# Low parts of the weights by an accumulating DMA in every fourth slab, in place of a VectorE subtraction

## The chip, the cores and the metric

One core of a Trainium2 chip runs the kernel. The metric is device time in microseconds (us) of one execution, lower is better. Engines are called as the profile calls them: PE (TensorE matmul), PEld (its weight loads), DVE (VectorE), ACT (ScalarE), POOL (GpSimd) and SP (SyncE, which here only issues DMAs).

## What is computed

One layer of a streaming encoder on 256 tokens of width 2048, all float32: a half-step feed-forward (SwiGLU), a mixer of latent attention and gated linear attention, cross-attention to 256 memory tokens, and a second half-step feed-forward.

```python
def swiglu(h, w_gate, w_up, w_down):
    return (jax.nn.silu(h @ w_gate) * (h @ w_up)) @ w_down
...
        x = x + 0.5 * swiglu(rmsnorm(x, ffn1_norm[l]), ffn1_w_gate[l], ffn1_w_up[l], ffn1_w_down[l])
        h = rmsnorm(x, mix_norm[l])
        z = h @ w_in[l]
...
        x = x + jnp.concatenate([o_mla, o_gla], axis=-1) @ w_out[l]
        x = x + memory_cross_attention(rmsnorm(x, mem_attn_norm[l]), rmsnorm(mem, mem_norm[l]), ...)
        x = x + 0.5 * swiglu(rmsnorm(x, ffn2_norm[l]), ffn2_w_gate[l], ffn2_w_up[l], ffn2_w_down[l])
```

D_MODEL is 2048 and D_FF 5632, so nearly all the time goes into products of 256 rows with large weight matrices, each weight read once from HBM.

## The kernel before

**Products in two parts.** To keep float32 accuracy, each operand is split into a high part (the value cast to float32r) and a low part (the value less its high part). A product is three matmuls: high x high, weights' low x high, weights' high x low. `gemm` (from L113) holds the activations' k-tiles of 128 as the stationary operand and streams 512 columns of weights; a k-tile of 1024 weight columns is worked off in 12 matmuls (two blocks of 128 tokens, two chunks of 512 columns, three products). In each pair the matmul with `wh` (high) stands directly ahead of the one with `wl` (low).

**Slabs.** `slab` (from L89) loads weights and splits them. For columns 1024 wide a slab is two k-tiles, called tile A and tile B below: 1 MB in one `raw` buffer, loaded by SP (L97; in the gate and up products two DMAs of 512 KB, in the others one of 1 MB). For each tile ACT casts `raw` to `wh` (L108) and DVE subtracts `wh` from `raw` into `wl` (L109):

```python
self.last_act = nc.scalar.copy(out=wh, in_=src)
self.last_dve = nc.vector.tensor_tensor(out=wl, in0=src, in1=wh.bitcast(F32), op=ALU.subtract)
```

**Buffers set the lead.** There are three `raw` buffers, and four each of `wh` and `wl`; a tile of 1024 columns takes one of each. So the split of a tile can begin when PE has finished the tile four before it, and PE has three more tiles to do before it needs the new one. A `raw` buffer is free for SP's load of three slabs later when both readers of tile B are done.

**Order.** The Tile framework traces the program and a scheduler fixes each engine's order of instructions; every engine works in that order, and semaphores hold an instruction until its operands and buffers are ready. SP's queue holds the loads, POOL's queue holds small operations for the norms (factors of 128 x 2 to 128 x 8 elements) and a few DMAs of small tables at the start and ahead of the mixer (`b_gate`, L462).

**Course of the program.** `ffn` runs 11 gate/up products of 8 slabs and four down products of 10 or 12 slabs; then comes the mixer (some narrower weights, and attention work woven in between the k-tiles), the cross-attention, and `ffn` again. The first product is special: its first two slabs hold one tile each, and the input's columns are loaded and transposed in between.

Of the kernel before, what the change touches and what calls it, by code (L numbers as in the profile page):

```python
# [10 lines left out]
F32 = mybir.dt.float32  # L11
# [4 lines left out]
ALU = mybir.AluOpType  # L16
AX = mybir.AxisListType

P = 128
# [5 lines left out]
CW = 512  # L25
EPS = 1e-6

H = 8
NOPE, ROPE, VD = 128, 64, 128
# [22 lines left out]
class Kernel:  # L52
    def __init__(self, ctx, tc, io):
        self.tc, self.nc, self.io = tc, tc.nc, io
        pool = lambda name, bufs, **k: ctx.enter_context(tc.tile_pool(name=name, bufs=bufs, **k))
        self.const = pool("const", 1)
        self.keep = pool("keep", 1)
        self.wraw = pool("wraw", 3)
        self.wspl = pool("wspl", 4)
        self.tmp = pool("tmp", 3)  # L60
        self.small = pool("small", 1)
        self.acc = pool("acc", 4, space=bass.MemoryType.PSUM)
        self.ps = pool("ps", 4, space=bass.MemoryType.PSUM)
        self.n_small = 0

# [8 lines left out]
    def rsqrt_mean(self, ss, n, scale=None):  # L74
        """(ss * scale + EPS) ** -0.5, elementwise on [P, n] (Pool)."""
        nc = self.nc
        ms = self.sm([P, n])
        nc.gpsimd.tensor_scalar(out=ms, in0=ss, scalar1=scale, scalar2=EPS, op0=ALU.mult, op1=ALU.add)
        r = self.sm([P, n])
        nc.gpsimd.tensor_tensor(out=r, in0=ms, in1=self.mhalf[:, :n], op=ALU.pow)  # L80
        return r
# [7 lines left out]
    def slab(self, segs, k0, nk, per):  # L89
        """k-tiles k0.. of the segments' columns: a (high, low) pair [P, width] for each; per of them at a time."""  # L90
        nc = self.nc
        width = sum(w for _, _, w in segs)
        flat = self.wraw.tile([P, 4 * CW], F32, name="raw")
        raw = flat[:, :nk * width].rearrange("p (j n) -> p j n", j=nk)
        off = 0
        for w, c0, n in segs:
            nc.sync.dma_start(  # L97
                out=raw[:, :, off:off + n],
                in_=w[k0 * P:(k0 + nk) * P, c0:c0 + n].rearrange("(j p) n -> p j n", p=P),
            )  # L100
            off += n
        parts = []
        for j in range(0, nk, per):
            m = min(per, nk - j)
            wh = self.wspl.tile([P, 2 * CW], F32R, name="wh")[:, :m * width]
            wl = self.wspl.tile([P, 2 * CW], F32R, name="wl")[:, :m * width]
            src = flat[:, j * width:(j + m) * width]
            self.last_act = nc.scalar.copy(out=wh, in_=src)  # L108
            self.last_dve = nc.vector.tensor_tensor(out=wl, in0=src, in1=wh.bitcast(F32), op=ALU.subtract)  # L109
            parts += [(wh[:, i * width:(i + 1) * width], wl[:, i * width:(i + 1) * width]) for i in range(m)]  # L110
        return parts

    def gemm(self, x, segs, chunks, ks, ahead=None, side=()):  # L113
        """x(k, b) -> (high, low) [P, P]; out[b][c] = sum_k x(k, b).T @ w[k][:, chunk c].

        side: generators of other work, a step of each traced after each k-tile."""
# [12 lines left out]
        while i < n:  # L129
# [9 lines left out]
            # one accumulator after the other in the last slab, so that they end apart  # L139
# [22 lines left out]
    def split_t(self, src, dst, j0, b, nj, g=None):  # L162
        """src [P tokens, nj * P] to dst's k-tiles j0.. for token block b; g: their columns in gains."""
# [31 lines left out]
    def norm_chunk(self, src, ht, ss, n, b, g, sq=True):  # L195
        """One [P, CW] chunk of the residual stream: its part of h.T and its sum of squares."""
        self.split_t(src, ht[n], 0, b, 4, g + 4 * n)
        if sq:
            self.sum_sq(src, ss[:, b, n:n + 1], CW)
# [32 lines left out]
    def load_rows(self, names, queue):  # L232
        """Norm weights, 128 to a row."""
# [9 lines left out]
    def turn_rows(self, rows, first, n):  # L243
        """... and to columns of gains."""
        t = self.bank()
        self.nc.tensor.transpose(out=t[:, :n], in_=rows[:n], identity=self.ident[:n, :n])
        return self.nc.vector.tensor_copy(out=self.gains[:, first:first + n], in_=t[:, :n])
# [5 lines left out]
    def setup_mix_body(self, pool):  # L253
# [7 lines left out]
        # products of the q and k norms' weights over the dimensions that aren't rotated  # L261
# [3 lines left out]
        # 0 where a key's chunk is not after the query's, within one block of 128  # L265
# [3 lines left out]
        # suffix[s, t] = 1 where s > t in the same chunk of 64; ends[s, c] = 1 where s is in chunk c  # L269
# [14 lines left out]
        # rotary tables: x * ta + swapped(x) * tb, each with the norm's weights in it  # L284
# [11 lines left out]
        # angles less whole turns (taken off part by part, each part exact), cos as a sine a quarter turn on  # L296
# [49 lines left out]
    def rotate(self, x, out, q, b, n):  # L346
        """x [P, n, ROPE] rotated (norm's weights included) into out [P, n, ROPE]."""
# [110 lines left out]
    def latent_input(self, lat, gate, x, z, r1, eds, dec):  # L458
        """Low-rank q and kv and the rotary key (in z), the gates' decays."""
# [25 lines left out]
        def steps():  # L485
# [27 lines left out]
            # log-sigmoid: min(y, 0) - log(1 + exp(-|y|))  # L513
# [7 lines left out]
            # the decay from a position to its chunk's end, and the chunk's  # L521
# [18 lines left out]
    def gla_qk(self, out, r1, gqt, eds):  # L540
        """q of gated linear attention, transposed; its k times the decay, in place of the decay."""
# [14 lines left out]
    def gla_states(self, gqt, eds, dec, gv, states, sso):  # L556
        """Chunk by chunk: states, and their outputs in place of gv; sums of squares of these."""
# [41 lines left out]
    def gla_gate(self, out, on, sso, r1, ogt):  # L599
        """Outputs of gated linear attention, normed and gated, transposed and split."""  # L600
# [33 lines left out]
    def latent_group(self, pool, g, z, r1, omt):  # L634
        """Four heads of latent attention, in two pairs: q, k and v, then what is left to do with them."""
# [34 lines left out]
        def steps():  # L670
            nsc = []
            ssq, ssk = self.sm([P, NB, 4]), self.sm([P, NB, 4])
            for b in range(NB):
# [12 lines left out]
                # minus the factor of the scores: both norms of q and the softmax's scale  # L686
# [10 lines left out]
                # k's factors: of the part from the low rank, of the rotary part  # L697
# [47 lines left out]
    def attend(self, scores, nscales, finish, causal, pts=None):  # L745
        """Heads one after the other, each a step behind the one before: scores and softmax; transposed; finish."""
# [11 lines left out]
    def soft_max(self, scores, nscale, causal):  # L758
        """One head's softmax over the keys: a tile [queries, keys] for each block of queries."""
# [19 lines left out]
    def soft_max_t(self, ss, pt, causal):  # L779
        """... transposed: pt's columns are (keys' block, query), without (1, block 0) when causal."""  # L780
# [9 lines left out]
    def weigh(self, v, pt, ot, k, causal):  # L790
        """One head's output, transposed and split, as k-tile k of ot."""
# [11 lines left out]
    def memory(self, pool, mt, mss):  # L803
        """mem, transposed and split, and its chunks' sums of squares."""
# [8 lines left out]
    def cross(self, pool, ht, mt, rm, r1, done):  # L813
# [18 lines left out]
        def head_norm(row, b, r, r2, scale):  # L832
            """The factors that turn a block's raw columns into normed ones, by head, times scale."""
# [60 lines left out]
    def run(self):  # L894
# [22 lines left out]
        def ahead(k):  # L917
            """Columns of x before the k-tiles that need them."""
# [64 lines left out]
```

## Time and profile before

| what | value |
|---|---|
| time, median of 2 runs | 1962.15 us (1961.65 and 1962.65) |
| span of the profiled execution (first to last instruction) | 1960.3 us |
| median less span | 1.9 us |
| PE busy | 1944.5 us, 99% |
| DVE busy | 1015.1 us, 52% |
| ACT busy | 903.7 us, 46% |
| POOL busy | 58.8 us, 3% |
| 16 DMA engines busy, SP's loads | 54.4% of the span |
| granted TensorE clock, mean | 0.999 |

How to read it: a busy share is that of an engine over the whole span. PE rows show the matmul's whole length, which overlaps with its neighbours; the distance from start to start is what a matmul costs in a row of many. A wait is put down to the engine whose work ended last before the waiting instruction began.

### The profile page before, as it was taken

How to read it: one execution, taken by the hardware profiler on the slowest of the kernel's cores; microseconds unless marked ns; L12 is line 12 of the kernel's file. 1: busy time of each engine (PE TensorE's matmuls, PEld its weight loads, DVE VectorE, ACT ScalarE, POOL GpSimd, SP SyncE). 2: the span in 40 equal slices, each digit the busy share in tenths (PEclk: the TensorE clock that was granted, in tenths of full speed). 3: DMA queues.
4: the chain of work that ended last, by engine and by line, in shares of the span. 5: the costliest groups of instructions: out<-in, count | busy, mean ns of one | idle time of the engine just before them, and what ended most of it. 6: DMA issues, size and time to landing. Idle time of an engine off the chain costs nothing.

```text
span 1960.3 us, 22343 instructions
## 1 busy us (share of the span) xinstructions
PE 1944.5 (99%) x8712; PEld 1583.4 (81%) x8712; DVE 1015.1 (52%) x1272; ACT 903.7 (46%) x1277; POOL 58.8 (3%) x114
## 2 busy tenths in 40 slices
PE   8999999999999999999999999999999999999999
PEld 6888888888888888788778878888888888888887
DVE  5555454444444455555566656444454445544443
ACT  5444443334444344665556666444444334444432
POOL 2000000000000000120100020000000000000000
PEclk9999999999999999999999999999999999999999
DMA  7555555555555555544335544655555555555563
GB/s 263 184 186 189 185 190 184 192 193 183 185 191 193 181 184 171 181 154 155 126 130 203 185 155 137 206 186 184 189 192 185 183 190 193 178 191 189 193 205 117
DMA packets 148074, 356.04 MB, mean 182 GB/s; under 512 B 11018, under 2 KB 11120, under 8 KB 147968
## 3 DMA queue, kind: packets, MB, share of 16 engines
q1 hardware_dynamic: 147360, 354.07, 54.4%
q8 instruction: 68, 1.11, 0.2%
q0 software_dynamic: 608, 0.55, 0.2%
q14 instruction: 38, 0.31, 0.0%
HBM read 352.48 MB, written 2.10 MB: 181 GB/s over the span
## 4 chain that ended last, share of the span: by engine, by line
PE 98%; ACT 1%; POOL 0%; DMA 0%; DVE 0%; issue 0%; SPq 0%; ACTq 0%
PE acc L123 93%; PE bank L168 2%; PE bank L732 0%; PE bank L587 0%; PE bank L568 0%; DMA raw<-in_ffn_w_up_dram 0%; PE bank L731 0%; PE bank L786 0%; PE bank L795 0%; ACT wh L108 0%; ACT junk L188 0%; PE bank L662 0%; PE bank L797 0%; PE bank L873 0%; POOL sm L80 0%
## 5 line engine op out<-in xcount | busy, mean ns | idle before, releaser
L109 DVE TENSOR_TENSOR wl<-raw,wh 128x1024 fp32r<-128x1024 f32 (+2 forms) x668 | 811.5, 1216 | 794.3 <-ACT wh L108 793.0
L108 ACT CAST wh<-raw 128x1024 fp32r<-128x1024 f32 (+2 forms) x668 | 696.4, 1048 | 926.9 <-PE acc L123 891.3
L123 PE MATMUL acc<-wh,hth 128*128 128x512 f32 (+1 forms) x1696 | 666.2, 393 | 2.8 <-ACT wh L108 2.8
L123 PE MATMUL acc<-wl,hth 128*128 128x512 f32 (+1 forms) x1696 | 658.8, 389 | 0.0
L123 PE MATMUL acc<-wh,htl 128*128 128x512 f32 (+1 forms) x1696 | 540.6, 388 | 0.0
L123 PEld LDWEIGHTS acc<-wh,hth 128*128 128x128 f32 x1696 | 319.3, 188 | 72.8 <-issue 3.7
L123 PEld LDWEIGHTS acc<-wh,htl 128*128 128x128 f32 x1696 | 318.2, 188 | 64.7
L123 PEld LDWEIGHTS acc<-wl,hth 128*128 128x128 f32 x1696 | 319.2, 188 | 63.0
L123 PE MATMUL acc<-wh,acth 128*128 128x512 f32 x704 | 279.9, 398 | 0.0
L123 PE MATMUL acc<-wl,acth 128*128 128x512 f32 x704 | 279.1, 396 | 0.0
L123 PE MATMUL acc<-wh,actl 128*128 128x512 f32 x704 | 227.2, 396 | 0.0
L123 PEld LDWEIGHTS acc<-wh,actl 128*128 128x128 f32 x704 | 132.6, 188 | 32.3
L123 PEld LDWEIGHTS acc<-wl,acth 128*128 128x128 f32 x704 | 132.6, 188 | 31.9
L123 PEld LDWEIGHTS acc<-wh,acth 128*128 128x128 f32 x704 | 132.6, 188 | 31.9
L379 DVE SCALAR_TENSOR_TENSOR t<-acc,sm,t 128x512 f32<-128x512 f32 x44 | 33.0, 750 | 51.6 <-PE acc L123 50.4
L377 ACT ACTIVATE t<-acc,sm 128x512 f32<-128x512 f32 x44 | 30.4, 691 | 49.7 <-PE acc L123 49.7
L182 DVE SCALAR_TENSOR_TENSOR htl<-bank,gains,hth 128x128 fp32r<-128x128 f32 x128 | 37.5, 343 | 10.1 <-ACT hth L179 9.7
L179 ACT ACTIVATE hth<-bank,gains 128x128 fp32r<-128x128 f32 x128 | 38.5, 389 | 7.3 <-PE bank L168 4.5
L168 PEld LDWEIGHTS bank<-ident,t 128*128 128x128 f32 x188 | 21.7, 140 | 13.1 <-DVE t L379 9.6
L395 DVE SCALAR_TENSOR_TENSOR xs<-acc,xs 128x512 f32<-128x512 f32 x32 | 21.5, 688 | 17.1 <-PE acc L123 17.1
L168 PE MATMUL bank<-ident,t 128*128 128x128 f32 x188 | 29.6, 279 | 0.2
L174 DVE TENSOR_TENSOR actl<-bank,acth 128x512 fp32r<-128x512 f32 x44 | 28.2, 681 | 0.0
(231 smaller groups left out, 985.4 us busy)
## 6 DMA issues: line engine op xcount, KB each, us to landing
raw<-in_ffn_w_down_dram SPq DMA_DIRECT2D x88, 1024.0 KB, 5.0
raw<-in_ffn_w_gate_dram SPq DMA_DIRECT2D x175, 512.0 KB, 3.8
raw<-in_ffn_w_up_dram SPq DMA_DIRECT2D x175, 512.0 KB, 4.7
raw<-in_w_in_dram SPq DMA_DIRECT2D x24, 1024.0 KB, 5.1
raw<-in_w_out_dram SPq DMA_DIRECT2D x16, 1024.0 KB, 5.2
raw<-in_w_in_dram SPq DMA_DIRECT2D x8, 832.0 KB, 4.6
raw<-in_mem_w_k_dram SPq DMA_DIRECT2D x4, 1024.0 KB, 5.1
raw<-in_mem_w_q_dram SPq DMA_DIRECT2D x4, 1024.0 KB, 5.1
```

What stands on the lines that cost most here:

```text
L108: self.last_act = nc.scalar.copy(out=wh, in_=src)
L109: self.last_dve = nc.vector.tensor_tensor(out=wl, in0=src, in1=wh.bitcast(F32), op=ALU.subtract)
L123: self.last_pe = nc.tensor.matmul(out=out[b][c][:, :w], lhsT=high, rhs=part[:, o:o + w], start=start, stop=stop)
L168: nc.tensor.transpose(out=t[:, j * P:(j + 1) * P], in_=src[:, j * P:(j + 1) * P], identity=self.ident)
L174: nc.vector.tensor_tensor(out=tl[:, j0:j0 + nj, bs], in0=tv, in1=hv.bitcast(F32), op=ALU.subtract)
L179: h = nc.scalar.activation(out=hv, in_=tv, func=AF.Copy, scale=gv)
L182: nc.vector.scalar_tensor_tensor(out=tl[:, j0 + j, bs], in0=tv, scalar=gv, in1=hv.bitcast(F32), op0=ALU.mult, op1=ALU.subtract)
L377: nc.scalar.activation(out=sg, in_=out[b][0], func=AF.Silu, scale=r)
L379: nc.vector.scalar_tensor_tensor(out=a, in0=out[b][1], scalar=r, in1=sg, op0=ALU.mult, op1=ALU.mult)
L395: nc.vector.scalar_tensor_tensor(out=xc, in0=out[b][c], scalar=0.5, in1=xc, op0=ALU.mult, op1=ALU.add)
```

## The change

In every fourth slab, counted over the whole program, of those that hold two tiles of 1024 columns, the low part is made in another way. ACT casts the raw weights a second time, negated, into `wl`; then a DMA issued from POOL adds the raw weights onto `wl` in SBUF. The sum, raw less its high part, is the same as the subtraction's. The other slabs keep the subtraction. The counter picks 78 of the 335 slabs, which is 156 tiles: 33 slabs in each feed-forward and 12 between them. In the first feed-forward they are mostly the third and seventh slab of a product, in the second the first and fifth. The diff also takes out comments, so that line numbers after it are 8 higher in the changed kernel.

```diff
         self.n_small = 0
+        self.n_slab = 0
...
         width = sum(w for _, _, w in segs)
+        self.n_slab += 1
+        by_dma = width == 2 * CW and nk == 2 and self.n_slab % 4 == 0
         flat = self.wraw.tile([P, 4 * CW], F32, name="raw")
...
             self.last_act = nc.scalar.copy(out=wh, in_=src)
-            self.last_dve = nc.vector.tensor_tensor(out=wl, in0=src, in1=wh.bitcast(F32), op=ALU.subtract)
+            if by_dma:
+
+                nc.scalar.mul(out=wl, in_=src, mul=-1.0)
+                nc.gpsimd.dma_start(out=wl, in_=src, accum_op=ALU.add)
+            else:
+                self.last_dve = nc.vector.tensor_tensor(out=wl, in0=src, in1=wh.bitcast(F32), op=ALU.subtract)
```

ACT's order in the middle of a gate/up product of the first feed-forward, before: one cast for each tile, two for each `raw` buffer (numbers tell buffers apart).

```order
L108 CAST wh_1004<-raw_1001 128x1024
L108 CAST wh_1008<-raw_1001 128x1024
L108 CAST wh_1039<-raw_1036 128x1024
L108 CAST wh_1043<-raw_1036 128x1024
L108 CAST wh_1074<-raw_1071 128x1024
L108 CAST wh_1078<-raw_1071 128x1024
```

ACT's order at the same place now; `raw_1081` is a slab of the new kind between two of the old.

```order
L111 CAST wh_1049<-raw_1046 128x1024
L111 CAST wh_1053<-raw_1046 128x1024
L114 ACTIVATE wl_1085<-raw_1081 128x1024
L111 CAST wh_1084<-raw_1081 128x1024
L114 ACTIVATE wl_1090<-raw_1081 128x1024
L111 CAST wh_1089<-raw_1081 128x1024
L111 CAST wh_1121<-raw_1118 128x1024
L111 CAST wh_1125<-raw_1118 128x1024
```

The negated cast to `wl` stands ahead of the cast to `wh` of the same tile, although the code names it second.

POOL's order from the end of the set-up to the b_gate table ahead of the mixer, before.

```order
L295 DMA g_rope<-in_mla_k_norm_dram 128x64
L78 TENSOR_SCALAR sm_486<-sm_484 128x2
L80 TENSOR_TENSOR sm_488<-sm_486,mhalf 128x2
L263 TENSOR_TENSOR gqk<-gains 128x1
L264 TENSOR_TENSOR gqk<-gains 128x1
L462 DMA b_gate<-in_gla_b_gate_dram 128x512
```

POOL's order from the same place now, up to the first slabs after the first norm's factors.

```order
L115 DMA wl_243<-raw_239 128x1024
L115 DMA wl_248<-raw_239 128x1024
L115 DMA wl_439<-raw_435 128x1024
L115 DMA wl_444<-raw_435 128x1024
L79 TENSOR_SCALAR sm5_490<-sm4_488 128x2
L81 TENSOR_TENSOR sm6_492<-sm5_490,mhalf_85 128x2
L115 DMA wl_631<-raw_627 128x1024
L115 DMA wl_636<-raw_627 128x1024
```

The accumulating DMAs stand in POOL's queue in the order of their slabs, with the small operations between them; there are 66 of them ahead of b_gate. SP's order is the same as before, and PE's differs in one place, in the first product, where in the first tile of the new kind two `wh` matmuls now stand ahead of two `wl` matmuls instead of each pair by itself.

## Rows read from the trace of the kernel before

**Rows 1.** The page's first part: busy us (share of the span) xinstructions.
```profile
PE 1944.5 (99%) x8712; PEld 1583.4 (81%) x8712; DVE 1015.1 (52%) x1272; ACT 903.7 (46%) x1277; POOL 58.8 (3%) x114
```

**Rows 2.** Groups by line and shape: busy us, mean ns of one, idle before, releasers.
```profile
L109 DVE TENSOR_TENSOR wl<-raw,wh 128x1024 fp32r<-128x1024 f32 x644 | 787.2, 1224 | 767.9 <-ACT wh L108 766.7
L108 ACT CAST wh<-raw 128x1024 fp32r<-128x1024 f32 x644 | 675.3, 1054 | 901.7 <-PE acc L123 868.4 <-DVE xs L395 19.3 <-issue 6.3
...
L377 ACT ACTIVATE t<-acc,sm 128x512 f32<-128x512 f32 x44 | 30.4, 691 | 49.7 <-PE acc L123 49.7
```

**Rows 3.** Waits by engine and line, over the span: us in total, times, longest.
```profile
ACT wh L108 <- PE acc L123: 891.3, 534, 3.9
...
DVE k L713 <- POOL sm L704: 13.7, 4, 4.1
```

**Rows 4.** ACT's timeline in a gate/up product: start us, length, idle before.
```profile
218.23 1.05 ACT L108 CAST wh<-raw 128x1024 fp32r<-128x1024 f32 x1 [1.67 <-PE acc L123]
220.95 1.05 ACT L108 CAST wh<-raw 128x1024 fp32r<-128x1024 f32 x1 [1.67 <-PE acc L123]
223.67 1.05 ACT L108 CAST wh<-raw 128x1024 fp32r<-128x1024 f32 x1 [1.67 <-PE acc L123]
```

**Rows 5.** DVE's timeline at the same place.
```profile
216.60 1.23 DVE L109 TENSOR_TENSOR wl<-raw,wh 128x1024 fp32r<-128x1024 f32 x1 [1.50 <-ACT wh L108]
219.32 1.23 DVE L109 TENSOR_TENSOR wl<-raw,wh 128x1024 fp32r<-128x1024 f32 x1 [1.50 <-ACT wh L108]
...
224.76 1.22 DVE L109 TENSOR_TENSOR wl<-raw,wh 128x1024 fp32r<-128x1024 f32 x1 [1.50 <-ACT wh L108]
```

**Rows 6.** PE's timeline where the tile cast at 218.23 us is used first.
```profile
226.19 0.39 PE L123 MATMUL acc<-wh,hth 128*128 128x512 f32 x1
226.42 0.39 PE L123 MATMUL acc<-wl,hth 128*128 128x512 f32 x1
```

**Rows 7.** SP's timeline: the load that is under way at 218.23 us.
```profile
217.85 0.37 SPq L97 DMA_DIRECT2D raw<-in_ffn_w_gate_dram  x1
218.26 0.47 SPq L97 DMA_DIRECT2D raw<-in_ffn_w_up_dram  x1
```

**Rows 8.** DMA issues by line: xcount, KB each, median us from issue to landing.
```profile
raw<-in_ffn_w_down_dram SPq DMA_DIRECT2D x88, 1024.0 KB, 5.0
raw<-in_ffn_w_gate_dram SPq DMA_DIRECT2D x175, 512.0 KB, 3.8
raw<-in_ffn_w_up_dram SPq DMA_DIRECT2D x175, 512.0 KB, 4.7
...
b_gate<-in_gla_b_gate_dram POOLq DMA_DIRECT2D x1, 256.0 KB, 3.4
```

**Rows 9.** DMA queues: packets, MB, share of 16 engines' span.
```profile
q1 hardware_dynamic: 147360, 354.07, 54.4%
```

**Rows 10.** POOL's timeline: the one 256 KB DMA that POOL issues.
```profile
755.95 0.64 POOL L462 DMA_DIRECT2D b_gate<-in_gla_b_gate_dram  x1 [469.36 <-PE acc L123]
```

**Rows 11.** The first product: ACT's cast of tile 4, PE's first use of its low part.
```profile
20.11 1.05 ACT L108 CAST wh<-raw 128x1024 fp32r<-128x1024 f32 x1 [1.50 <-DMA raw<-in_ffn_w_up_dram]
...
24.29 0.39 PE L123 MATMUL acc<-wl,hth 128*128 128x512 f32 x1
```

**Rows 12.** The mixer's first kv product, one slab: ACT's two casts, PE's two first uses.
```profile
848.85 1.05 ACT L108 CAST wh<-raw 128x1024 fp32r<-128x1024 f32 x1 [1.14 <-PE acc L123]
850.97 1.05 ACT L108 CAST wh<-raw 128x1024 fp32r<-128x1024 f32 x1 [1.07 <-PE acc L123]
...
855.25 0.40 PE L123 MATMUL acc<-wl,zkvth 128*128 128x512 f32 x1
...
855.94 0.39 PE L123 MATMUL acc<-wl,zkvth 128*128 128x512 f32 x1
```

**Rows 13.** Busy us (x) of PE, PEld, DVE, ACT, POOL in one stretch; PEclk, DMA share, GB/s.
```profile
196.00:294.00 98.00, 97.99 (x439) 80.40 (x438) 48.91 (x45) 41.36 (x43) 1.25 (x2) 1.00 0.56 187
```

## Prediction

> **What bounds the kernel now.** I read the page's busy shares first. PE is busy 1944.5 of 1960.3 us [rows 1], so all that any other engine could give back is PE's idle time, 15.8 us or 0.8%. The stretch from 196 to 294 us shows the steady state: PE 97.99 of 98 us, granted clock 1.00, DMA engines 0.56 busy [rows 13]. The waits say the same from the other side: ACT's cast waits 891.3 us in all for PE to give up a buffer [rows 3], and DVE's subtraction waits for that cast [rows 2]. The splitters run as far ahead as four buffers allow and then sit idle. A cheaper subtraction therefore buys nothing; the question is whether the new way of making `wl` still arrives in time.
>
> The timeline gives the time there is. Casts follow each other by 2.72 us, which is PE's time for a tile (220.95 less 218.23) [rows 4]. The tile cast from 218.23 us is needed in its low part at 226.42 us [rows 6]: 8.19 us, which is three tiles of 2.72 us (8.16) and a little. Today its `wl` is ready at 219.32 + 1.23 = 220.55 us [rows 5], 5.87 us early. I call the start of tile A's cast c0 (here 218.23); tile B's is c0 + 2.72, and its `wl` is needed by c0 + 10.91.
>
> **The change part by part.** *Removed:* 156 subtractions of 1.224 us [rows 2], 191 us of DVE, none of it on PE's path. Worth 0.
>
> *Added on ACT:* 156 negated casts. No row shows one; by the plain cast of that shape it is 1.05 us, by the 128x512 ACTIVATE of 0.691 us taken twice 1.38 us [rows 2]. It is nearest to the cast: 1.05. That makes ACT 903.7 + 164 = 1068 us, 54%. In a tile's 2.72 us it has 1.67 us idle [rows 4], so the second cast fits. It stands ahead of the `wh` cast in ACT's order, so `wh` is ready at c0 + 2.1 instead of c0 + 1.05, and is needed at 226.19, c0 + 7.96: hidden by 5.9 us. The negated cast can begin when the `wl` buffer is free, at c0 or a little before; it ends at c0 + 1.05 and POOL issues the DMA at c0 + 1.1.
>
> *Added on the DMA engines:* 156 accumulating DMAs of 512 KB, SBUF to SBUF. This is the term on which all hangs, and no row shows such a DMA. I split it into a fixed part and engine time W. For plain loads 512 KB land after 3.8 us and 1024 KB after 5.0 [rows 8], so 512 KB cost 1.2 us and the fixed part is 2.6. From the queue's share, 54.4% of 1960.3 us is 1066 us for 354.07 MB [rows 9], 1.6 us for 512 KB. POOL's own 256 KB land after 3.4 us [rows 8], 0.64 of it the issue [rows 10]; less 0.6 to 0.8 of engine time the fixed part is about 2.7. So a plain copy would have W of 1.2 to 1.6. An accumulating one must also read what it adds to, two reads for each write; with the reads one after the other W is 2.4 to 3.2. The far bound charges b_gate's 3.4 us wholly to its size: 6.8. I take 2.8, the middle of the doubled range, because that is the work the DMA has to do if nothing else holds it.
>
> The Trainium skill, "Collectives: The Full Stack", section "The bandwidth ceiling", says that a DMA that adds runs at half the rate of one that copies because it reads two sources, and that the addition itself costs nothing (32.35 against 62.28 GB/s). No run here shows it yet; by its ratio of 1.93 W would be an estimated 2.7 and the forecast the same, and it is what speaks against an addition that is slow in itself.
>
> *Whether it arrives:* the DMA engines are shared with SP's loads. The load under way at c0 was issued at 217.85 and 218.26; by the medians its second half lands 4.7 us later, at 222.96 = c0 + 4.73 [rows 7, 8]. If the engines then never idle, both accumulations are done by c0 + 4.73 + 2W. Tile A lands by about c0 + 4.73 + 2.8 = 7.5 (needed 8.19), tile B by c0 + 10.3 (needed 10.91). B is the tighter one: spare 0.6 us. B is late when W is above 3.09; from there each such slab stops PE for 2W - 6.18 us. If B did not queue at all, it would land at c0 + 2.72 + 1.1 + 2.7 + 2.8 = 9.3.
>
> *Next in line:* `raw` is now held until B's DMA has landed, c0 + 10.3 instead of 222.04 + 1.22 = c0 + 5.0. SP's load of three slabs later then lands at about c0 + 10.3 + 5.1 = 15.4, and its first cast can begin at c0 + 3 x 5.44 = 16.3. Hidden by 0.9 us, and behind that the 5.87 us of the other slabs. DMA engine time grows by 156 x 2.8 = 437 us to 1503 of 1960.
>
> *POOL:* each DMA holds its queue until its negated cast is done. Behind it stand the small operations of the norms; in the mixer DVE waited 13.7 us for these in four waits [rows 3]. Twelve slabs lie there, and an operation behind a pair is held by at most about a tile's time. I count 0, with 12 x 2.7 = 32 us as the bound.
>
> *Tight places:* tile 4 of the first product has 24.29 - 20.11 = 4.18 us from cast to use [rows 11]; the new way needs 1.1 + 2.7 + 2.8 = 6.6, so PE waits about 2.4 us. In the mixer's first kv product the tiles have 6.40 and 4.97 us [rows 12]; A lands at 855.45, 0.2 late, and B a W later, at 858.25, 2.3 late. With W of 1.4 it would be 1 us for both places together.
>
> *Sum:* 78 slabs x 0 + 2.4 + 2.3 = about 5 us on a span of 1960.3 us; the runs lie 1.9 us above the span, so 1962.15 + 5 = 1967 us.
>
> **The rivals.** *The accumulation is slow (slower than before).* One mechanism at one place: tile B's DMA ends after c0 + 10.91, PE stands at the `wl` matmul. For it speaks that my price lies only 0.3 under the point where it begins, and that no row bounds it from above but the one at 6.8; against it, that the engines have room (0.56 busy [rows 13]). At W = 4.2, three times a plain copy, each slab loses 2.2 us: 78 x 2.2 + 5 = 177, so 2140 us. At 6.8 it is 7.4 us a slab, 579 us, about 2545, and the DMA engines are by then full on their own (1066 + 156 x 6.8 = 2127 us). The 2% line (39 us, 0.5 us a slab) is passed at W = 3.35.
>
> *The change gives time back.* DVE is relieved of 191 us, but it is idle half the span and PE waits for it almost nowhere. At most PE's idle 15.8 us: 1946 us. That it does what it says and it does not matter is my forecast; this is the bound on being wrong in the good direction.
>
> *DVE holds up the issue.* If POOL could not write its descriptors while a subtraction runs, an issue would slip by up to 1.23 us, B's spare of 0.6 would turn into a loss of 0.6, and 78 x 0.6 = 49 us would give 2016. Against it: the subtraction before ends at 217.83, c0 - 0.4, and the next, of the slab after, starts at 224.76, c0 + 6.5 [rows 5]; the issues fall at c0 + 1.1 and c0 + 3.8, between them. The Trainium skill, "SBUF — State Buffer", section "Who interferes with whom", has such a block for DVE's two-port modes and takes subtractions of two tensors out of it; no run here shows either.
>
> **How the numbers follow.** The sum with W below 3.35: 0.55, of which 0.03 is a small gain. W from 3.35 to about 4.2, 2001 to 2140 us: 0.22, the slipped issue included. Slower than that: 0.22. Below 1960 at all: 0.01 beyond the 0.03. A measurement of this kernel tells about 2% from no change, so faster is 0.01 (PE's work alone forbids it), same 0.56, slower 0.43. The range goes from 1960, no loss at all and a little gained, to 2140, the tripled copy, and leaves out 0.22 above; the likeliest case's own range is 1960 to 2001.
>
> **What would show it.** Right: PE at 99% busy and its first `wl` matmul in a fourth slab never released by a DMA, except at the two tight places; about 191 us less DVE, 164 us more ACT; accumulating DMAs that land within 5.5 us when undisturbed and within 7 us in the worst case; SP's waits released by a DMA in every fourth slab. Wrong: waits of PE for `wl` DMAs in all 78 slabs, landings of 8 us and more for tile B. A landing time of the accumulation is the number that decides.

## The result, and the profile after

The changed kernel takes 1995.16 us (1995.0 to 1995.33) against 1962.15: a ratio of 1.0167, 95% interval 1.0151 to 1.0184. That is 33.0 us more, less than the 2% by which the chances were given, but far outside the scatter of the runs, and far above the forecast's 5 us, though inside its range of 1960 to 2140 us. The profiled execution spans 1993.2 us, 32.9 more than the one before.

From the page, the busy engines and the two DMA queues that carry data (packets, MB, share of the 16 engines' span), as [rows 1, 9] gave them before:

```profile
PE 1956.2 (98%) x8712; PEld 1586.1 (80%) x8712; DVE 827.7 (42%) x1116; ACT 1047.9 (53%) x1433; POOL 188.0 (9%) x270
...
q1 hardware_dynamic: 147360, 354.07, 52.9%
q0 software_dynamic: 23072, 82.35, 20.9%
```

The groups of the new instructions, and the issues of the new DMA (KB each, median us to landing), as in [rows 2, 8]:

```profile
L115 POOL DMA_DIRECT2D wl<-raw x156 | 132.8, 854 | 1554.9 <-ACT wl L114 1426.7
L114 ACT ACTIVATE wl<-raw 128x1024 fp32r<-128x1024 f32 x156 | 165.7, 1062 | 143.4 <-PE acc L131 126.5
...
wl<-raw POOLq DMA_DIRECT2D x156, 512.0 KB, 6.4
```

DVE lost 187 us and ACT gained 144, as forecast in kind. A tile's accumulation costs 0.209 x 1993.2 / 156 = 2.67 us of the DMA engines: the W of the prediction, which took 2.8. It lands 6.4 us after its issue in the median. PE's matmul lines are L131 now, L123 before; all line numbers behind the edit moved by 8.

The waits over the whole span (us in total, times, longest) show where PE lost time:

```profile
PEld acc L131 <- DMA wl<-raw: 32.1, 23, 4.0
PE acc L131 <- DMA wl<-raw: 22.4, 19, 3.6
```

PE and its weight loads are two views of one stop, so they aren't added. PE stood 19 times at a matmul with `wl`, for 22.4 us, in 78 slabs. Each stop costs a little more than its wait. PE's timeline at one of them (start us, length, idle before):

```profile
261.98 0.39 PE L131 MATMUL acc<-wh,hth 128*128 128x512 f32 x1
263.25 0.50 PE L131 MATMUL acc<-wl,hth 128*128 128x512 f32 x1 [0.89 <-DMA wl<-raw]
263.59 0.40 PE L131 MATMUL acc<-wh,hth 128*128 128x512 f32 x1
```

From 261.98 to 263.59 two matmuls started in 1.61 us where two steps of 0.23 are normal: 1.15 lost, of which the wait shows 0.89. The other 0.26 us have two parts: the wait is counted from the end of a row that is 0.39 long, 0.16 after the next matmul would have started, and the first step behind the stop takes 0.34 us in place of 0.23. Taken for all 19 stops, an estimate, this gives 22.4 + 19 x 0.26 = 27.3 us. The rest is the clock. Three stretches lie just behind the three longest stops, which end at 28.14 us (3.6 us), 124.42 us (2.31) and 881.76 us (2.29, tile B of the mixer's first kv product); with us, busy time of PE, PEld, DVE, ACT and POOL, granted clock, DMA share and GB/s:

```profile
27.00:31.00 4.00, 2.86 (x8) 2.30 (x9) 0.78 (x1) 0.00 (x0) 0.00 (x0) 0.72 0.69 136
...
124.00:128.00 4.00, 3.58 (x9) 2.89 (x10) 0.27 (x1) 0.00 (x0) 0.00 (x0) 0.57 0.21 43
...
882.00:886.00 4.00, 4.00 (x12) 3.08 (x12) 2.24 (x5) 1.87 (x8) 0.00 (x0) 0.57 0.76 249
```

At 0.57 in place of 1.00 a stretch of 4 us loses 1.7 us of work; three of them make 5.1 us (the first is only partly inside its window). The clock stood at the lower of its two levels, 1.2 GHz, for part of each, after PE had waited for a `wl` tile. By the means of the whole executions it is 0.003 x 1993 = 6 us (granted clock 0.999 before, 0.996 after). Together 27.3 + 5.1 = 32.4 of the 32.9 us. Matching the two traces matmul by matmul says the same without an estimate: PE falls back by 32.6 us within twelve matmuls of these stops, the lower clock included, and by 0.3 us in all the rest.

**Which tiles are late.** The stops were matched to their slabs by counting the matmuls in the trace. Thirteen of the 19 lie in the first feed-forward, and each is a tile A: the one in the first product (3.6 us), and twelve of the thirteen slabs that stand third in a later product, 0.4 to 1.0 us each but for two at 1.75 and 2.31. Slabs that stand seventh lose nothing. Tile B, which the prediction held for the tighter one, is late once in the whole kernel (the mixer's kv product, 2.29 us). The two kinds side by side, each in the timeline of its window (PE's rows left out); first a slab that stands seventh and loses nothing:

```profile
229.48 1.22 DVE L117 TENSOR_TENSOR wl<-raw,wh 128x1024 fp32r<-128x1024 f32 x1 [1.50 <-ACT wh L111]
230.66 1.06 ACT L114 ACTIVATE wl<-raw 128x1024 fp32r<-128x1024 f32 x1 [1.21 <-PE acc L131]
230.73 0.37 SPq L100 DMA_DIRECT2D raw<-in_ffn_w_gate_dram  x1
231.14 0.47 SPq L100 DMA_DIRECT2D raw<-in_ffn_w_up_dram  x1
...
232.01 0.85 POOL L115 DMA_DIRECT2D wl<-raw  x1 [19.14 <-ACT wl L114]
```

Then the next one, third in its product, which stops PE until 263.25:

```profile
252.03 1.28 DVE L182 TENSOR_TENSOR actl<-bank,acth 128x512 fp32r<-128x512 f32 x2
253.23 1.21 DVE L117 TENSOR_TENSOR wl<-raw,wh 128x1024 fp32r<-128x1024 f32 x1
253.56 1.06 ACT L114 ACTIVATE wl<-raw 128x1024 fp32r<-128x1024 f32 x1 [1.13 <-PE acc L131]
254.51 0.37 SPq L100 DMA_DIRECT2D raw<-in_ffn_w_gate_dram  x1
...
254.92 0.47 SPq L100 DMA_DIRECT2D raw<-in_ffn_w_up_dram  x1
254.92 0.85 POOL L115 DMA_DIRECT2D wl<-raw  x1 [19.35 <-ACT wl L114]
```

The chain of waits of this window (start, us, what) passes through that DMA, from its issue to its landing at 263.21:

```profile
254.92 8.29 DMA wl<-raw
```

In the first, c0 is 230.66 and the load under way was issued at c0 + 0.1 and, by its issue records, was complete at 235.89; tile A landed at 238.34, 2.45 us behind it. In the second the previous slab's last subtraction stands behind the evacuation of the previous product (`actl`, 252.03), so the raw buffer comes free and the load is issued 0.9 us later, at c0 + 0.95. Its second half also takes 5.9 us in place of 4.8, landing at 260.78 = c0 + 7.2. Tile A lands at 263.21, again 2.43 us behind it, and 1 us too late. In 75 of the 78 slabs a load lands between the end of tile A's issue and A's own landing; A follows it by 2.43 us in the median (2.35 to 3.44 for the middle eight tenths), which is close to W.

The queues in three stretches of that slab show why it is the load's end that counts. First 256 to 259 us, then 259 to 260.8, then 260.8 to 263.2; POOL had issued tile A's DMA at 254.92 (packets reach over the edges of so short a stretch, so a share can pass 100%):

```profile
q1 hardware_dynamic: 396, 0.78, 91.5%
...
q0 software_dynamic: 55, 0.23, 62.6%
q1 hardware_dynamic: 119, 0.21, 38.1%
...
q0 software_dynamic: 139, 0.50, 106.0%
```

From 256 to 259 us the load has the engines alone and the accumulation moves nothing; when the load's packets run out, the accumulation has them alone. Here they don't share. This is the theory that the runs below test: **the accumulation starts when the load in flight is done, and a slab is late where that load is late.** The rivals: the POOL DMA has a long fixed price of its own; its traffic slows the rest; ACT's second cast is not free.

### The profile page after: what moved, and what is told of

The parts are those of the page before. It is cut to its first block, busy times and chain, and to the rows that moved or that the text cites. A ratio compares the mean times of both kernels' runs of the same rounds, so it can differ in the third digit from the quotient of the medians.

```text
span 1993.2 us, 22974 instructions
## 1 busy us (share of the span) xinstructions
PE 1956.2 (98%) x8712; PEld 1586.1 (80%) x8712; DVE 827.7 (42%) x1116; ACT 1047.9 (53%) x1433; POOL 188.0 (9%) x270
## 4 chain that ended last, share of the span: by engine, by line
PE 73%; DMA 17%; issue 6%; ACT 2%; SPq 1%; DVE 1%; POOL 0%; POOLq 0%; ACTq 0%; DVEq 0%
PE acc L131 69%; DMA wl<-raw 11%; DMA raw<-in_ffn_w_up_dram 4%; DMA raw<-in_ffn_w_down_dram 1%; PE bank L176 1%; SPq L100 1%; ACT wl L114 1%; ACT wh L111 1%; DVE wl L117 0%; PE bank L740 0%; PE bank L595 0%; PE bank L576 0%; PE bank L739 0%; PE bank L794 0%; PE bank L670 0%
## 5 line engine op out<-in xcount | busy, mean ns | idle before, releaser
L117 DVE TENSOR_TENSOR wl<-raw,wh 128x1024 fp32r<-128x1024 f32 (+2 forms) x512 | 620.2, 1213 | 891.0 <-ACT wh L111 890.1
L131 PE MATMUL acc<-wl,hth 128*128 128x512 f32 (+1 forms) x1696 | 662.2, 391 | 13.4 <-DMA wl<-raw 13.2
L131 PE MATMUL acc<-wh,hth 128*128 128x512 f32 (+1 forms) x1696 | 667.1, 394 | 1.9 <-ACT wh L111 1.9
L131 PE MATMUL acc<-wh,htl 128*128 128x512 f32 (+1 forms) x1696 | 542.5, 390 | 0.0
L131 PEld LDWEIGHTS acc<-wl,hth 128*128 128x128 f32 x1696 | 320.3, 189 | 81.6 <-DMA wl<-raw 18.6
L131 PEld LDWEIGHTS acc<-wh,hth 128*128 128x128 f32 x1696 | 320.2, 189 | 71.6 <-issue 3.7
L131 PEld LDWEIGHTS acc<-wh,htl 128*128 128x128 f32 x1696 | 319.3, 189 | 65.2
L131 PE MATMUL acc<-wl,acth 128*128 128x512 f32 x704 | 279.8, 397 | 4.8 <-DMA wl<-raw 4.8
L131 PE MATMUL acc<-wh,acth 128*128 128x512 f32 x704 | 279.8, 397 | 0.0
L115 POOL DMA_DIRECT2D wl<-raw x156 | 132.8, 854 | 1554.9 <-ACT wl L114 1426.7
L114 ACT ACTIVATE wl<-raw 128x1024 fp32r<-128x1024 f32 x156 | 165.7, 1062 | 143.4 <-PE acc L131 126.5
L131 PE MATMUL acc<-wh,actl 128*128 128x512 f32 x704 | 227.2, 396 | 0.0
L131 PEld LDWEIGHTS acc<-wl,acth 128*128 128x128 f32 x704 | 132.6, 188 | 39.4 <-DMA wl<-raw 7.8
L131 PEld LDWEIGHTS acc<-wh,actl 128*128 128x128 f32 x704 | 132.6, 188 | 32.4
L131 PEld LDWEIGHTS acc<-wh,acth 128*128 128x128 f32 x704 | 132.6, 188 | 31.6
```

The source lines that it names most:

```text
L114: nc.scalar.mul(out=wl, in_=src, mul=-1.0)
L115: nc.gpsimd.dma_start(out=wl, in_=src, accum_op=ALU.add)
L131: self.last_pe = nc.tensor.matmul(out=out[b][c][:, :w], lhsT=high, rhs=part[:, o:o + w], start=start, stop=stop)
```

## The experiments

Each run was timed beside the kernel before on the same chip (1962.1 to 1962.3 us in every set).

**Without the DMA, with the second cast.**

```diff
-                nc.gpsimd.dma_start(out=wl, in_=src, accum_op=ALU.add)
+                self.last_dve = nc.vector.tensor_tensor(out=wl, in0=src, in1=wh.bitcast(F32), op=ALU.subtract)
```

> The negated cast stays in every fourth slab, but the DMA behind it is gone and DVE's subtraction writes over its result as before the change (the 156 extra casts are work without use). My theory: what PE loses is its wait for accumulating DMAs; the extra cast, 156 x 1.06 = 166 us of ACT, is hidden. So 1962 to 1965 us. Rival, ACT's second cast holds up the splitters: then a part of the 33 us stays, 1970 us and more.

1960.5 us, ratio 0.9993 (0.9983 to 1.0002). ACT's 166 us are hidden; the loss is the DMA's.

**The DMA's traffic without a reader.** The subtraction is back everywhere; the accumulation goes onto the raw tile.

```diff
+            self.last_dve = nc.vector.tensor_tensor(out=wl, in0=src, in1=wh.bitcast(F32), op=ALU.subtract)
             if by_dma:
-                nc.scalar.mul(out=wl, in_=src, mul=-1.0)
-                nc.gpsimd.dma_start(out=wl, in_=src, accum_op=ALU.add)
-            else:
-                self.last_dve = nc.vector.tensor_tensor(out=wl, in0=src, in1=wh.bitcast(F32), op=ALU.subtract)
+                nc.gpsimd.dma_start(out=src, in_=wh.bitcast(F32), accum_op=ALU.add)
```

> The subtraction is back in all slabs, without a negated cast, and PE reads its result; in every fourth slab POOL still issues an accumulating DMA of the same size, from wh onto the raw tile after both have been used, a transfer whose result nobody reads. My theory: the loss is PE's wait for wl alone, not the traffic, nor the raw buffers that are held longer: 1962 to 1966 us. Rival, the traffic itself costs (slower loads, later raw buffers, stalled splitters): 1980 us and more.

1962.8 us, ratio 1.0008 (0.9999 to 1.0018), with 156 accumulating DMAs on the engines:

```profile
L114 POOL DMA_DIRECT2D raw<-wh x156 | 132.7, 852 | 1537.9 <-DVE wl L112 1378.3
```

Neither the traffic, nor POOL's issues, nor raw buffers held longer cost anything measurable. What costs is that PE waits for the result.

**A plain copy in place of the addition.**

```diff
-                nc.gpsimd.dma_start(out=wl, in_=src, accum_op=ALU.add)
+                nc.gpsimd.dma_start(out=wl, in_=src)
```

> The DMA copies the raw weights over the negated cast instead of adding them, so the low part is wrong in every fourth slab; everything else, its issue on POOL and its waits, is as in the changed kernel. By the queue's share the accumulation takes 2.67 us of engine time for a tile; a plain copy should take about half, 1.3 us. My theory: the copy starts on the DMA engines only when SP's load in flight is done, and lands about 1.3 us earlier than the accumulation. In the slabs that lose 0.4 to 1.0 us this is enough, in the four that lose 2 us half goes, the first product keeps about 2: 1967 us, 1964 to 1973. Rival, a POOL DMA has a long fixed part whatever its bytes: the landing moves by less than 0.5 us and 1985 us or more stays.

1968.3 us, ratio 1.0034 (1.0021 to 1.0047), in the expected place. The queue's line:

```profile
q0 software_dynamic: 23072, 82.35, 11.5%
```

0.115 x 1964.7 / 156 = 1.45 us for a tile, against 2.67 with the addition: a ratio of 1.84. Tile A lands 1.28 us behind the load's end in the median (2.43 before), and only the first product, one kv tile and one later slab still stop PE (2.6, 1.2 and 0.2 us). Halving the engine time removed most of the loss; a long fixed price would have stayed.

**Half of the slabs, two ways.** In `e3_mod8_4` the condition reads `n_slab % 8 == 4`, in `e4_mod8_0` it reads `n_slab % 8 == 0`.

```diff
-        by_dma = width == 2 * CW and nk == 2 and self.n_slab % 4 == 0
+        by_dma = width == 2 * CW and nk == 2 and self.n_slab % 8 == 4
```

> Only every eighth slab (number 4, 12, 20, ...) keeps the accumulating DMA; the others of every fourth go back to the subtraction. In the first feed-forward these are the slabs that stand third in their product (rows 4 and 5 of it), whose splits come right behind the evacuation of the product before. My theory: PE's gaps of these slabs sum to 15 us in the changed kernel and two of its three added stretches at half clock lie here (3.4 us): 1981 us, 1978 to 1986, more than half of the 33 us for half of the DMAs. Rival, each DMA costs a share by its traffic: half of 33 us, 1978 to 1979, here and in the complementary kernel alike.

> The complement: only slabs 8, 16, 24, ... keep the accumulating DMA, in the first feed-forward those that stand seventh in their product. My theory: in the changed kernel PE's gaps at these sum to 7 us (the mixer's first kv product 2.8, the attention output product 1.6, and three of the second feed-forward), with one added stretch at half clock (1.7 us): 1971 us, 1966 to 1974. Rival, cost by traffic: the same as in the other half, about 1978.

1984.5 us (1.0116, 1.0101 to 1.0131) and 1970.8 us (1.0043, 1.0028 to 1.0058): 22.4 and 8.7 us for the same number of DMAs, 31.1 of the 33 us together. The price goes by the place, not by the traffic. PE's waits between 40 and 840 us in the changed kernel, in `e3_mod8_4` and in `e4_mod8_0`:

```profile
PE acc L131 <- DMA wl<-raw: 11.5, 12, 2.3
```

```profile
PE acc L131 <- DMA wl<-raw: 10.5, 12, 1.7
```

```profile
PE acc L131 <- DMA wl<-raw: 0.5, 1, 0.5
```

**The same slabs moved by two.**

```diff
-        by_dma = width == 2 * CW and nk == 2 and self.n_slab % 4 == 0
+        by_dma = width == 2 * CW and nk == 2 and self.n_slab % 4 == 2
```

> The same 78 or so DMA pairs, moved by two slabs: numbers 2, 6, 10, ... in place of 4, 8, 12. In the first feed-forward these stand first and fifth in their product, and in the second third and seventh, the other way round than in the changed kernel. My theory: being third in a product is what makes a slab late (the load in flight is issued later there), so the waits move from the first feed-forward to the second and the total stays near: 1985 to 2000 us, PE's waits for wl between 20 and 1000 us fall to few, and those in the second feed-forward rise to one for each of its eleven products. Rival, the first feed-forward itself (cold start, its loads) is slow: the waits there stay, or all go.

1995.8 us, ratio 1.0176 (1.0159 to 1.0193): the total stays and the waits move house. First 40 to 780 us, the first feed-forward behind its first product, where the changed kernel had 11.5 us in 12 waits; then 1230 to 1990 us, the second, where it had 2.9 us in 3:

```profile
PE acc L131 <- DMA wl<-raw: 1.4, 2, 0.9
...
PE acc L131 <- DMA wl<-raw: 12.3, 13, 2.2
```

All 13 in the second feed-forward are third slabs of a product (0.5 to 2.2 us), ten of its eleven gate/up products among them. Being third is the condition, not the feed-forward. That the total stays so exactly is in part chance: the first product waits 0.5 us in place of 3.6, and the mixer and the cross-attention 9.3 us in place of 4.4.

**The slab two behind not loaded.** This was to take away the load in flight (`fast` holds for slabs of two tiles of 1024 columns).

```diff
+        if fast and self.n_slab % 4 == 2 and self.raw_w == width:
+            nc.gpsimd.memset(flat[:, :1], 0.0)
+            flat = self.raw_flat
+        else:
...
```

> The slab two behind each one with accumulating DMAs is not loaded (of the wide slabs alone): it splits the raw weights of the slab before it once more, so its products are wrong, and 78 of the loads, those that were under way while the accumulations ran, are left out. Its buffer is only touched by a small POOL memset. My theory: the accumulation waits for the load in flight to be done; without that load it lands about 4.5 us after its issue for tile A in place of the median of 6.4, and PE no longer waits outside the first product and the mixer's first kv product (4 to 6 us): 1966 to 1970 us. Rival, the accumulation is late by its own fixed part or by its issue on POOL: it lands as late as now, and 1985 us or more stays.

2003.5 us, ratio 1.0212 (1.0197 to 1.0228): a miss, and the edit was at fault. The following slab's load took the empty place: at the seventh slabs it is issued 0.3 us behind c0, and the landing stays (median 6.7 us). At the third slabs it comes behind tile A's DMA, which makes this run of use. The timeline there, SP's and POOL's rows:

```profile
256.28 0.85 POOL L122 DMA_DIRECT2D wl<-raw  x1 [19.36 <-ACT wl L121]
...
257.27 0.37 SPq L106 DMA_DIRECT2D raw<-in_ffn_w_gate_dram  x1
...
259.00 0.84 POOL L122 DMA_DIRECT2D wl<-raw  x1 [1.76 <-ACT wl L121]
```

And the queues in the stretches from 258 to 259.5 and from 262 to 264.5 us:

```profile
q0 software_dynamic: 77, 0.32, 123.0%
...
q1 hardware_dynamic: 374, 0.71, 89.9%
```

Issued 1 us ahead of the load, tile A has the engines to itself and the load waits for it; tile B, issued behind the load, waits for the load, lands 8.7 us after its issue and stops PE by 1.3 us. So here the DMA engines favour neither kind: the transfer that was issued first is done first.

**The load in flight made short.** The load keeps its place and its issue and brings an eighth of the columns.

```diff
+            r = n // 8 if width == 2 * CW and nk == 2 and self.n_slab % 4 == 2 else n
-                out=raw[:, :, off:off + n],
-                in_=w[k0 * P:(k0 + nk) * P, c0:c0 + n].rearrange("(j p) n -> p j n", p=P),
+                out=raw[:, :, off:off + r],
+                in_=w[k0 * P:(k0 + nk) * P, c0:c0 + r].rearrange("(j p) n -> p j n", p=P),
+            if r < n:
+                nc.vector.memset(raw[:, :, off + r:off + n], 0.0)
```

> The load of the slab two behind each one with accumulating DMAs, the load that is under way while they run, brings only an eighth of its columns (64 of 512, or 128 of 1024); DVE fills the rest of the raw tile with zeros, so these slabs' products are wrong. The load's place, its waits and its issue stay. The run before this one was to show the same by leaving the load out, but there the next slab's load took its place under way. My theory: the accumulation's data moves only when the load in flight is done; a load of 128 KB instead of 1024 KB is done some 3 us earlier, so tile A lands 4.5 to 5 us after its issue (median now 6.4), and PE waits for wl only in the first product and the mixer: 1968 us, 1963 to 1975. Rival, the accumulation is late by a fixed part of its own, by its issue on POOL or by POOL's place behind other work: the landing stays at 6 us and more and 1985 us or more stays.

1968.0 us, ratio 1.0028 (1.0017 to 1.0039), as the theory said. The issue line, and the landings of all 156 (us, min/median/max):

```profile
wl<-raw POOLq DMA_DIRECT2D x156, 512.0 KB, 4.6
...
DMA to landing us min/median/max: 4.5/4.6/8.2
```

6.4 us became 4.6 with nothing changed in the accumulation. What is left are the first product (2.65 us) and tile B of the kv product (2.34 us). With the lower clock that stands behind each, these two cover the 6 us.

**`wl` used later.** In these slabs (not in a product's last slab) PE takes `wh` for both token blocks first, then `wl`. The first `wl` matmul of a tile moves from second place to ninth, which is seven matmuls of 0.23 us, 1.6 us more time (the expectation counts eight and 1.8).

```diff
-                    product(b, c, wl, xh)
+                    if not late:
+                        product(b, c, wl, xh)
+                if late and b == NB - 1:
+                    for b2 in range(NB):
+                        for c in cs:
+                            product(b2, c, wl, x(ks[i + j], b2)[0])
```

> As the changed kernel, but in the slabs with accumulating DMAs (not in a product's last slab) PE does the matmuls with wh of both token blocks first and those with wl behind them, so the first need of a wl tile lies eight matmuls, 1.8 us, later. My theory: nearly all slabs are late by less than 1 us, four by about 2; these waits go, the first product keeps about 1.8, the kv product is its product's last slab or near it and may keep its share: 1966 us, 1963 to 1972. Rival, the loss lies in something other than the arrival of wl (the POOL issue, clock, loads): 1985 us or more stays.

1973.5 us, ratio 1.0064 (1.0049 to 1.0079), 1.5 us over the expected range. Of the third slabs one is still late (0.34 us). The first product (2.25) and kv (0.5 and 2.3) remain, 5.7 us of waits in all, and the mean granted clock is 0.997, 0.002 x 1971 = 4 us: the clock's part was left out of that expectation.

**`wl` used later, and no DMA in the tight places.**

```diff
-        self.by_dma = by_dma = width == 2 * CW and nk == 2 and self.n_slab % 4 == 0
+        self.by_dma = by_dma = width == 2 * CW and nk == 2 and self.n_slab % 4 == 0 and self.long
+        self.long = n > 4 and not ahead
```

> The later use of wl from the run e7_wl_last, and the accumulating DMAs left out of the two tight places: the first product and the mixer's products of two to four k-tiles make their low part by subtraction again (147 tiles or so keep the DMA). In e7_wl_last PE still lost 5.7 us at wl tiles, 5.1 of it in these places, and one or two stretches at half clock behind them. My theory: with these gone nothing is left of the 33 us, and nothing is gained either, since DVE was not what PE waited for: 1963 us, 1960 to 1967. Rival, relieving DVE by 180 us gives PE something back once the late tiles are cured: below 1955 us.

1965.7 us, ratio 1.0016 (1.0006 to 1.0025). Four matmuls still wait for `wl`, where the changed kernel had 19:

```profile
PE acc L131 <- DMA wl<-raw: 2.2, 4, 1.0
```

DVE is relieved of 179 us:

```profile
PE 1946.6 (99%) x8712; PEld 1582.7 (81%) x8712; DVE 836.3 (43%) x1124; ACT 1042.1 (53%) x1425; POOL 184.4 (9%) x262
```

And still nothing is gained: 3.4 us of loss are left (4.7 in the profiled execution), and the four stops make 2.2 + 4 x 0.26 = 3.2 of them (the granted clock is 1.00 in the 3 to 4 us behind each). So the expectation was right in the time and in that PE gains nothing, but not in that nothing would be left of the stops. No version of this change that was run beats the kernel before.

**Twice as many.**

```diff
-        by_dma = width == 2 * CW and nk == 2 and self.n_slab % 4 == 0
+        by_dma = width == 2 * CW and nk == 2 and self.n_slab % 2 == 0
```

> The change made twice as often, in every second slab (about 312 tiles). At 2.67 us of engine time for a tile the accumulations take 833 us and with the loads' 1050 us the DMA engines are 95% full. My theory: tile A of a slab still waits for the load in flight, and now the loads are pushed behind the accumulations of the slab before, so nearly each of the 156 slabs is late by 1 us or more: 2100 us, 2050 to 2300. Rival, only the third place in a product is late, whatever stands around it: about twice the 33 us, 2025 to 2035.

2365.4 us, ratio 1.2056 (1.2036 to 1.2076): the direction was right and the size was missed by 265 us. The queues of the page, the issues of the new DMA, and the waits of PE and of SP's queue:

```profile
q1 hardware_dynamic: 147360, 354.07, 47.3%
q0 software_dynamic: 44960, 162.05, 34.7%
...
wl<-raw POOLq DMA_DIRECT2D x308, 512.0 KB, 9.6
```

```profile
PE acc L131 <- DMA wl<-raw: 283.5, 149, 4.3
...
SPq L100 <- DMA wl<-raw: 1867.2, 192, 15.6
```

The DMA engines are not full (47.3 + 34.7 = 82%) and W is the same, 0.347 x 2362.7 / 308 = 2.66 us. But nearly every slab now stops PE: 283.5 + 149 x 0.26 = 322 us, and the granted clock of 0.962 costs 0.037 x 2363 = 87 more, 409 us together, where 402 were lost. A ring has closed. SP's next loads wait for a raw buffer until the accumulation has landed (1867 us of waits), and the next accumulation waits for those loads. The chain of waits shows the first half:

```profile
744.32 10.40 DMA wl<-raw
...
756.28 13.39 DMA raw<-in_ffn_w_up_dram
```

The DMA from 744.32 lands at 754.71, and SP then issues the loads of two slabs in a row, the last at 756.28. For the second half, the accumulation issued at 727.44 moves its first packet at 732.11, when the first of two such loads is ending (landed 732.37), and from there it runs beside the second load. That three ordinary slabs between let the loads catch up, and one doesn't, is how I read this; it was not tried by itself. The expectation counted the engines' time alone, not this ring.

## Why the prediction was right or wrong

*PE is the bound, and relief of DVE is worth nothing:* right. DVE lost 187 us and nothing came back, not even in `e12_roomy`, where four waits of 2.2 us in all are left and account for most of the loss.

*ACT's second cast is hidden:* right; 1.06 us each against 1.05, and `e1_cast_only` costs nothing.

*The engine time W = 2.8:* right, 2.67 measured. The doubling of a plain copy held: 1.84 times. The Trainium skill, "Collectives: The Full Stack", section "The bandwidth ceiling", has a ratio of 1.93 between the rates of a collective (a transfer among several cores) that copies and of one that adds; the trace agrees within 5%. So the accumulation is not slow in itself, and the rival that began at W = 3.09 did not happen. The fixed part was taken too large: undisturbed, an accumulation lands 4.5 us after its issue, 1.9 more than W, not 2.7.

*The landing at c0 + 7.5 for A and c0 + 10.3 for B, so B is the tighter:* **this is the step that failed.** The sum, the load's end and then W, was the right one; `e11_short_load` and `e10_no_load` show that. But the load's end, c0 + 4.73, was read at one slab, a seventh one, and put in for all 78. There it holds well enough in the changed kernel too (235.89 is c0 + 5.2, A at c0 + 7.7, no stop). In a third slab the load is issued 0.9 us later and its second half takes 1.1 us longer, so the end is c0 + 7.2 and A lands at c0 + 9.65, 1 us too late. The later issue could be read in the trace of before, at the third slab of the next product, where DVE's subtraction stands behind the evacuation (`actl`) as well; [rows 4 to 7] were all taken from the middle of a product:

```profile
239.15 1.28 DVE L174 TENSOR_TENSOR actl<-bank,acth 128x512 fp32r<-128x512 f32 x2
240.35 1.21 DVE L109 TENSOR_TENSOR wl<-raw,wh 128x1024 fp32r<-128x1024 f32 x1
...
241.16 1.05 ACT L108 CAST wh<-raw 128x1024 fp32r<-128x1024 f32 x1 [1.60 <-PE acc L123]
...
241.63 0.37 SPq L97 DMA_DIRECT2D raw<-in_ffn_w_gate_dram  x1
242.04 0.47 SPq L97 DMA_DIRECT2D raw<-in_ffn_w_up_dram  x1
```

With c0 = 241.16 the load's second half is issued at c0 + 0.88, not c0 + 0.03, and the prediction's own 4.7 and 2.8 us then put A at c0 + 8.4, past the need at c0 + 8.19. So 78 x 0 should have been worked out place by place. The other part, the 1.1 us, stands in no row of before, and its cause is open; with the measured 2.43 us in place of 2.8 the later issue alone would have left A just in time, at c0 + 8.0. It takes both to make the stops of about 1 us. The twelve late third slabs of the first feed-forward are 11.5 of the 22.4 us, the largest part. And B has more room than A, not less: its landing follows A's by 2.5 us in the median and its need by 2.72, where the sum put 2.8 between the landings. A stop at A moves B's need back besides.

*The raw buffers and SP's late loads are hidden:* right; `e6_unread` holds them as long (SP waits 799 us for these DMAs, 787 in the changed kernel) at no cost. `e9_every_second` shows where it ends.

*POOL's small operations, 0:* right; DVE's wait for POOL in the mixer is 13.8 us, as in [rows 3].

*The tight places, 2.4 and 2.3 us:* the places were right; they lost 3.6 us (first product) and 0.5 + 2.3 (kv). But both sums let the DMA wait for nothing on the engines, and in both it stood behind a load. In the first product this was the input's (`xs`, landed at 25.66; A landed at 28.10, 2.44 us behind it), in the kv product the one landed at 876.03 (A at 878.47, again 2.44). So the failed step is in these terms too, and that the second came out near is in part luck. What was left out besides is that a stop of PE can bring the lower clock with it: 1.7 us behind each of the three longest, 5 of the 33 us.

*DVE holds up the issue:* not seen. 148 of POOL's 156 issues start 0.3 us behind their negated cast; the other eight start 1 to 4.2 us behind it and stop PE nowhere. The 22 issues during which DVE works take 0.85 us in the median, like the rest.

The sum's 5 us should have been 33: 27 in stops, 5 in clock. The claim that PE waits "only at two tight places" is wrong by 16 stops, that of landings "within 7 us in the worst case" by 2.7 us (the longest takes 9.7). That 1995 us lies in the range, and even in the 1960 to 2001 us that went with W below 3.35, is luck: there the time above 1967 belonged to a W between 3.09 and 3.35 that stops tile B in every one of the 78 slabs. W was 2.67, and what stopped was tile A, in some slabs.

## What to carry to other kernels

A DMA put in place of an engine's work must be timed against the transfer that is ahead of it on the DMA engines, at every kind of place in the loop: the start of a product, where the evacuation of the last one delays the splits and so the loads, is another place than its middle. A margin of 0.7 us that is read at one place is no margin. And relief of an engine that is not waited for buys nothing even when nearly all the side effects are cured (`e12_roomy`), so such a change can only lose.

## What the runs showed of the hardware

An accumulating DMA of 512 KB within SBUF takes 2.67 us of the DMA engines where a copy takes 1.45, and lands 4.5 us after its issue at the earliest; 0.85 us of that is POOL's issue. With the load in flight cut short (`e11_short_load`) tile A's first packet moves 1.42 us after the issue in the median, in the changed kernel 2.91: the rest of the 2.91 is waiting.

The transfer that was there first was served first, whole, whichever queue it was on: the load in the changed kernel (91.5% to 0), whose first half was issued 0.4 us ahead of POOL's DMA; the accumulation in `e10_no_load`, issued 1 us ahead (no packet of the load from 258 to 259.5 us). The Trainium skill, "DMA: Bandwidth & Descriptors", section "Queues, rings and completion order", says that an engine goes round between its queues packet by packet. In these stretches the trace does not agree, and the measurement decides. In `e9_every_second` there is sharing: from 733 to 738 us, with a slab's load (second half 0.7 us later) and an accumulation issued within 0.3 us of each other behind an earlier load, the queues stand like this, nearly packet for packet (215 to 232), as that section of the Trainium skill says:

```profile
q0 software_dynamic: 215, 0.82, 81.6%
q1 hardware_dynamic: 232, 0.44, 26.2%
```

What decides between the two ways was not tried. Also open is why a load issued at the same moment as POOL's DMA takes about 1.1 us longer, though the accumulation moves nothing meanwhile, and why single transfers now and then land 2 us later still; four of the 19 stops (1.6 to 2.3 us, not counting the first product and kv) come from such.
